# A hybrid decoder layer on Trainium2: the sums of the seven-product form as identity products on TensorE, and a new order of compression, keys and queries

## The chip, the cores and the metric

The kernel runs on one core of one Trainium2 chip. The metric is the device time of one execution in microseconds (us). The kernel before was run three times; the median is compared. The trace is of one profiled execution of the same program.

## The reference, cut to what matters

One decoder layer over 1024 tokens of width 1024, in float32:

- a SwiGLU feed-forward block (inner width 2816) on a normalised and modulated input, `u = norm(h) * a + b` with a and b from a conditioning vector, added to the residual stream h;
- a mixer on the next such u: one wide projection `u @ w_in` (queries, keys and values of sparse attention with compressed, selected and windowed branches, queries, keys, values and a gate of retention, and two merge gates), then attention (8 heads in 4 pairs), retention (8 heads in chunks of 128 tokens), and `sigmoid(ga) * (o_nsa @ w_nsa_up) + sigmoid(gb) * (o_ret @ w_ret_up)`, projected by `w_out` and added to h;
- a second feed-forward block and a final norm.

Every large product must come out at float32 quality. The kernel holds each operand as a high part (rounded to the matmul's fp32r format) and a low part (the rest), and makes one product as three: high by high, high by low, low by high (`mm3`, L275).

## The kernel before, in words

Activations lie transposed, 128 features in the partitions and tokens along the row, in two halves of 512 tokens. `u[hf]` is a pair of tiles (high, low) of 8 row blocks d for the half hf. A PSUM bank takes 512 float32 columns; `psA` has two tiles of two banks, `psO` four of one.

**The seven-product form.** Large projections are made as a 2 by 2 block product with seven block products in place of eight (a Strassen form). It needs sums of quarters of u. `combine` (L287) makes them: with b11, b21 the upper and lower four row blocks of the first half and b12, b22 those of the second, T3 = b22 - b12, T2 = b22 - t1 with t1 = b12 - b11, T4 = b21 - T2, and T1 = t1. A quarter is first put together from its high and low parts (L296, three of four on VectorE, one on GpSimd), then added (L307 and L310 on VectorE, L308 and L312 on GpSimd), then split again by `put`: ScalarE copies the high part (L300), VectorE subtracts for the low part (L301). The tile of T1 replaces b12, so that `put` comes after all plain products that read b12. `combine` runs three times: ahead of the first feed-forward block, of the mixer and of the second block. I call these places the transitions. Before each one the norm is applied: `norm_u` (L233) multiplies on VectorE (L240), adds the shift and rounds on ScalarE (L246), and makes the low part on VectorE (L248) or, for every second row block, and for every one in the first block, on GpSimd (L251, L252). Around the transition a few column tiles are made by plain products: `plain` (L498) and its gated evacuation (L478; VectorE L482 or L485), `first_proj` (L988; its gates' copy is L998) and `plain_t` (L1004). After it the weight sets follow: `wset` and `wset_n` split and combine weights (L334 to L344), `seven` (L380) empties the products (L391 to L416).

**The mixer's order** (`run`, L1491 to L1521): the first retention set, retention of four heads (`ret_core`) woven with the second retention set, retention of the other four woven with the further sets (keys, queries, merge gates), then `compress`, then sets up to the last, `keys` (L1017) woven with the last set. Keys, queries and values go through HBM: each is loaded into a staging buffer, copied to its high part on ScalarE and its low part is subtracted on VectorE (L1029 and L1030, L1056 and L1057, L1043 and L1044). Q0, the values and Q1 are loaded after the last set, ahead of `attention` (L1074).

**Attention** works per pair of heads p and token block i from 7 down to 0: scores on TensorE (L1070, L1071), mask and maximum on VectorE (L1117), exponentials on ScalarE (L1132), scaling on GpSimd (L1137), transposes on TensorE (L1159), a split on ScalarE and VectorE (L1162, L1163), products with the values (L1173). Between them stand steps of `ret_up` (L1201): first four loads of the retention output, split on ScalarE and GpSimd (L1198, L1199) through one staging buffer (t4h), then sixteen groups of 12 products. `FILL` (L31) says at which blocks a step is taken. `merge` (L1227) then makes `o_nsa @ w_nsa_up` and combines it with loads of the gates and the retention part (d_gab, 32 loads), and `out_seven` (L595) projects; its low parts are L679, its copies L678, its loads of h L633.

**What sets the order.** The code states an order, and a planner that simulates the engines (it is part of the language's compiler) may take a later instruction of a queue first when an earlier one is not ready by its own costs; `high_priority` moves instructions ahead. Each engine then works its queue in that fixed order. All DMAs but a few go through the queue of SP.

Of the kernel before, what the change touches and what calls it, by code (L numbers as in the profile page):

```python
# [17 lines left out]
P = 128  # L18
# [12 lines left out]
FILL = ((6, 5, 4), (6, 5, 3, 2, 1, 0), (6, 5, 4, 3, 2, 1), (7, 6, 5, 4, 3))  # L31
# [21 lines left out]
class Layer:  # L53
# [4 lines left out]
    def setup(self):  # L58
# [4 lines left out]
        nc.sync.dma_start(self.ident, I["k_ident"])  # L63
        self.ones = const.tile([P, P], F32, name="ones")
# [149 lines left out]
    def norm(self, i, hf, u, pool, state):  # L214

        ps = self.psA.tile([P, 2, H2], F32, name="s")
        with self.tc.high_priority():
            bc = self.norm_bc(hf, pool, ps[:, 0, :], ps[:, 1, :], state)
        u.append(self.half(hf))
        for d in range(KD):  # L220
            yield
            self.norm_u(i, hf, u, d, bc)
# [10 lines left out]
    def norm_u(self, i, hf, u, d, bc, shift=True, pool_lo=2):  # L233
# [13 lines left out]
        if d % pool_lo:  # L247
            nc.vector.scalar_tensor_tensor(ul, t, b, f32(uh), op0=ALU.add, op1=ALU.subtract)  # L248
        else:
            t2 = self.tmp.tile([P, H2], F32, name="tg", bufs=2)  # L250
            nc.gpsimd.tensor_scalar(t2, t, b, 1.0, op0=ALU.add, op1=ALU.mult)  # L251
            nc.gpsimd.tensor_sub(ul, t2, f32(uh))  # L252
# [34 lines left out]
    def combine(self, u, pool, us, first):  # L287


        nc = self.nc  # L290
        T2, T3, T4 = [tuple(pool.tile([P, 4, H2], F32R, name="t%d%s" % (i, x)) for x in "hl") for i in (2, 3, 4)]

        t1 = first.tile([P, 4, H2], F32, name="t1f")

        def quarter(eng, r, c, d, t):
            eng.tensor_add(t, f32(u[c][0][:, 4 * r + d, :]), f32(u[c][1][:, 4 * r + d, :]))  # L296
            return t

        def put(dst, d, t):
            nc.scalar.copy(dst[0][:, d, :], t)  # L300
            nc.vector.tensor_sub(dst[1][:, d, :], t, f32(dst[0][:, d, :]))  # L301

        for d in range(4):
            x = [self.tmp.tile([P, H2], F32, name=t, bufs=2) for t in ("t2", "tn", "tg")]
            b11, b12 = quarter(nc.vector, 0, 0, d, t1[:, d, :]), quarter(nc.vector, 0, 1, d, x[0])
            b22, b21 = quarter(nc.vector, 1, 1, d, x[1]), quarter(nc.gpsimd, 1, 0, d, x[2])
            nc.vector.tensor_sub(b11, b12, b11)  # L307
            nc.gpsimd.tensor_sub(b12, b22, b12)  # L308
            put(T3, d, b12)
            nc.vector.tensor_sub(b22, b22, b11)  # L310
            put(T2, d, b22)
            nc.gpsimd.tensor_sub(b21, b21, b22)  # L312
            put(T4, d, b21)
        yield
        T1 = tuple(x[:, 0:4, :] for x in u[1])
        for d in range(4):
            put(T1, d, t1[:, d, :])
        b11, b21 = [tuple(x[:, r:r + 4, :] for x in u[0]) for r in (0, 4)]
        us += [b11, b21, tuple(x[:, 4:8, :] for x in u[1]), T4, T1, T2, T3]
# [147 lines left out]
    def ffn(self, i, w_in, w_out, u, state, reg, first=None, norms=(), then=iter(()), side=()):  # L467
# [30 lines left out]
        def plain(wab, hf, f):  # L498
            pp = self.psA.tile([P, 2, H2], F32, name="s")
            for x in range(2):  # L500
                self.mm_u(pp[:, x, :], wab[x], u, hf)
            gated([pp[:, 0, :], pp[:, 1, :]], hf, f)
# [3 lines left out]
        def seven():  # L506
# [5 lines left out]
            comb = self.combine(u, pool, us, pool)  # L512
# [43 lines left out]
        else:  # L556
            ws = []
            for f in fs:
                self.sub = (nc.gpsimd, nc.vector)[f]
                ws.append(load(f))  # L560
# [456 lines left out]
    def keys(self, pool):  # L1017
# [3 lines left out]
        for b in range(2):  # L1021
            src = self.d_k[b].rearrange("(g d) t -> d g t", g=2)
            for hf in range(2):
                s = slice(hf * H2, (hf + 1) * H2)
                a = self.stage()
                for r in range(2):
                    nc.sync.dma_start(a[64 * r:64 * r + 64], src[:, :, s])
                kh, kl = self.Kh[b][:, :, s], self.Kl[b][:, :, s]
                nc.scalar.copy(kh, a)  # L1029
                nc.vector.tensor_sub(kl, a, f32(kh))  # L1030
# [15 lines left out]
    def queries(self, p, pool, stage):  # L1046
        nc = self.nc
        src = self.d_q[p].rearrange("(j d) t -> d j t", j=2)
        Q = self.Q[p] = pool.tile([P, 2, T], F32R, name="t3" + "hl"[p % 2])
        lr = slice(64, 128) if p < 2 else slice(0, 64)  # L1050
        for hf in (1, 0):
# [5 lines left out]
            nc.vector.tensor_sub(Q[lr, :, s], a[lr], f32(Q[lr, :, s]))  # L1057

# [15 lines left out]
    def attention(self, pool, sp, stage, psS, psT, psO, fill):  # L1074
# [7 lines left out]
        for p in range(4):  # L1082
            g = p // 2
            for i in range(NT - 1, -1, -1):
                if p and p < 3 and i == 7:
                    self.queries(p + 1, sp, stage)
                elif i in FILL[p]:
# [139 lines left out]
    def merge(self, onsa, mix, pool):  # L1227
        nc = self.nc
        wn = self.I["w_nsa_up"][0].rearrange("(k p) n -> p k n", p=P)
        for d in range(KD):  # L1230
            w = self.weights(wn[:, :, d * P:(d + 1) * P], [P, 4, P])
            for hf in range(2):
                s = slice(hf * H2, (hf + 1) * H2)
                a = self.tmp.tile([P, H2], F32, name="tn", bufs=2)
                nc.sync.dma_start(a, self.d_gab[d, :, s])
                b = pool.tile([P, H2], F32, name="ga", bufs=2)
# [58 lines left out]
    def run(self):  # L1295
# [56 lines left out]
        def first():  # L1352
# [51 lines left out]
            for hf in range(2):  # L1404
                for d in range(KD):
                    self.norm_u(0, hf, u, d, bcs[hf], True, 1)
# [32 lines left out]
        c_t = ExitStack()  # L1439
        sp = pool(c_n, "sevenm", "right")  # L1440
        us = []
        comb = self.combine(u, sp, us, pool(c_t, "sevenf", "right"))
# [5 lines left out]
        c_t.close()  # L1448
# [33 lines left out]
        def sets():  # L1482
# [3 lines left out]
            for d in range(KD):  # L1486
                if d == KD - 1:
                    yield "late"
# [4 lines left out]
        fill = itertools.chain(more, sets())  # L1493
        for r in range(2):
# [3 lines left out]
        with ExitStack() as c1:  # L1498
            weave(self.compress(self.keep, pool(c1, "cmp", "right")), fill, 4)
        kv = pool(c_n, "kv", "right")  # L1500
        for x in fill:
            if x == "late":
                break
        weave(self.keys(kv), fill, 2)
# [6 lines left out]
        self.Q = {}  # L1511
        self.queries(0, sp, self.stage)
# [6 lines left out]
        self.queries(1, sp, stage)  # L1519
# [79 lines left out]
```

## Time and profile before

| | |
|---|---|
| Runs (median of 3, lowest to highest) | 2398.12 us (2394.84 to 2399.73) |
| The profiled execution's own time | 2396.19 us |
| Its span, first to last instruction | 2394.4 us |
| Mean granted TensorE clock | 0.973 of full speed |
| Matmuls | 11563 |
| HBM read, written | 216.45 MB, 69.73 MB |

How to read it: the span is what the trace covers; the execution's own time is 1.8 us longer. An engine is busy while an instruction of its kind is under way; matmuls overlap, so that a busy TensorE is not one at its peak, and the count of matmuls in a stretch says more. The clock has two levels, 1.2 and 2.4 GHz; a granted clock between them is a mean over a stretch.

The stages by the trace: setup and opening of the first block to 130 us, its sets to 480, its output projection to 730, the transition to the mixer to 820, the mixer to 1260, attention to 1560, merge and output projection to 1695, the transition to the second block to 1780, its sets to 2145, output projection and final norm to the end.

### The profile page before, as it was taken

The numbers are of one execution on the slowest core, as the hardware profiler recorded it, in microseconds if no ns is written. First come the engines' busy times: TensorE is split into PE (matmuls) and PEld (weight loads), VectorE is DVE, ScalarE is ACT, GpSimd is POOL, SyncE is SP. The second block draws the span as 40 slices with busy tenths as digits, with TensorE's granted clock in tenths as the row PEclk, the third lists the DMA queues.
The fourth block names the chain that finished last, engine by engine and source line by source line (L and its number), as shares of the span: only waits on it lengthen the run. The fifth ranks groups of instructions, "written<-read, shape, count | busy, mean of one in ns | idle before, by whom it ended". The sixth has DMA issues, their size and how long they took to land.

```text
span 2394.4 us, 32603 instructions
## 1 busy us (share of the span) xinstructions
PE 2263.2 (95%) x11563; PEld 1904.2 (80%) x11563; DVE 1774.0 (74%) x2858; ACT 1054.5 (44%) x1904; POOL 1025.2 (43%) x784
## 2 busy tenths in 40 slices
PE   7799999999997899999997999999879999999998
PEld 5578888887886899887886889877668888887886
DVE  7888888668888855676757887849895555558888
ACT  4432222235774322123437876816432222235676
POOL 3755454534104544565315444530464444445202
PEclk8999999999998999999998999999899999999999
DMA  9135656374204344353544121380212222236311
GB/s 350 56 98 171 199 170 201 103 242 137 88 1 136 93 129 125 91 158 117 168 127 114 54 85 63 134 257 2 106 58 83 88 80 80 80 131 224 103 45 70
DMA packets 248886, 288.31 MB, mean 120 GB/s; under 512 B 14852, under 2 KB 169236, under 8 KB 248724
## 3 DMA queue, kind: packets, MB, share of 16 engines
q1 hardware_dynamic: 248608, 286.19, 37.6%
q8 instruction: 91, 1.49, 0.3%
q14 instruction: 71, 0.58, 0.1%
q10 hardware_dynamic: 116, 0.05, 0.0%
HBM read 216.45 MB, written 69.73 MB: 120 GB/s over the span
## 4 chain that ended last, share of the span: by engine, by line
PE 37%; DVE 6%; DMA 3%; ACT 2%; issue 1%; POOL 1%; SPq 0%; DVEq 0%; ACTq 0%; POOLq 0%
PE po L281 17%; PE po L758 5%; PE s L758 5%; PE ot L1173 3%; PE pt L1159 2%; PE s L281 2%; PE s L1070 1%; PE s L1071 1%; DMA tn<-d_gab 1%; DVE wp L679 1%; PE pt L862 1%; PE ot L1170 0%; POOL mix L1241 0%; POOL tg L251 0%; DVE pl L1163 0%
## 5 line engine op out<-in xcount | busy, mean ns | idle before, releaser
L281 PE MATMUL po<-u0h,wp 128*128 128x512 f32 x944 | 306.1, 395 | 7.3 <-DVE gates L998 4.9
L281 PE MATMUL po<-u1h,wp 128*128 128x512 f32 x880 | 282.0, 391 | 3.4 <-DVE bias L544 2.2
L758 PE MATMUL po<-wp 128*128 128x512 f32 x1128 | 268.7, 394 | 10.5 <-DVE wp L679 7.8
L758 PEld LDWEIGHTS po<-wp 128*128 128x128 f32 x1128 | 214.2, 190 | 59.3 <-DVE wp L679 10.5
L758 PE MATMUL s<-wp 128*128 128x512 f32 x1056 | 249.1, 392 | 4.1 <-DVE wp L679 2.5
L758 PEld LDWEIGHTS s<-wp 128*128 128x128 f32 x1056 | 199.1, 189 | 47.3 <-DVE wp L679 4.0
L334 ACT CAST wp<-S 128x1024 fp32r<-128x1024 f32 x98 | 103.0, 1051 | 300.4 <-PE po L281 296.4
L281 PEld LDWEIGHTS po<-u0h,wp 128*128 128x128 f32 x944 | 179.5, 190 | 46.9 <-DVE gates L998 5.1
L281 PEld LDWEIGHTS po<-u1h,wp 128*128 128x128 f32 x880 | 165.1, 188 | 40.2 <-DVE bias L544 2.6
L281 PE MATMUL po<-u0l,wp 128*128 128x512 f32 x472 | 186.1, 394 | 0.0
L463 POOL TENSOR_TENSOR t<-t,t 128x512 f32<-128x512 f32 x38 | 56.3, 1483 | 299.9 <-DVE t L407 187.9
L281 PE MATMUL po<-u1l,wp 128*128 128x512 f32 x440 | 172.5, 392 | 2.5 <-DVE u1l L243 2.5
L335 DVE TENSOR_TENSOR wp<-S,wp 128x1024 fp32r<-128x1024 f32 x98 | 158.3, 1615 | 15.5 <-ACT wp L334 15.3
L334 ACT CAST wp<-raw 128x1024 fp32r<-128x1024 f32 x98 | 82.1, 837 | 186.0 <-PE po L281 177.6
L341 POOL TENSOR_TENSOR S<-raw 128x512 f32<-128x512 f32 x49 | 69.2, 1413 | 153.2 <-DMA raw<-w_in 47.3
L281 PE MATMUL po<-t2h,wp 128*128 128x512 f32 x392 | 131.6, 396 | 2.2 <-ACT t2h L300 1.4
L281 PE MATMUL po<-t4h,wp 128*128 128x512 f32 x392 | 131.6, 396 | 1.3 <-DVE tn L399 0.7
L281 PE MATMUL po<-t3h,wp 128*128 128x512 f32 x392 | 131.8, 397 | 0.2 <-DVE t L395 0.2
L335 DVE TENSOR_TENSOR wp<-raw,wp 128x1024 fp32r<-128x1024 f32 x98 | 115.3, 1177 | 12.1 <-ACT wp L334 11.9
L395 DVE TENSOR_TENSOR t<-tn,po 128x512 f32<-128x512 f32 x57 | 39.0, 685 | 111.0 <-issue 76.9
L1163 DVE TENSOR_TENSOR pl<-pt,ph 128x512 fp32r<-128x512 f32 (+2 forms) x160 | 96.8, 619 | 11.6 <-ACT ph L1162 10.9
L251 POOL TENSOR_SCALAR tg<-tn,mod 128x512 f32<-128x512 f32 x32 | 36.6, 1149 | 160.6 <-DVE tn L240 151.5
(467 smaller groups left out, 6022.2 us busy)
## 6 DMA issues: line engine op xcount, KB each, us to landing
raw<-ffn_w_in SPq DMA_DIRECT2D x88, 512.0 KB, 4.3
raw<-ada_w SPq DMA_DIRECT2D x56, 512.0 KB, 4.3
raw<-w_in SPq DMA_DIRECT2D x40, 512.0 KB, 4.1
d_g<-t SPq DMA_DIRECT2D x50, 256.0 KB, 2.2
d_h<-hT SPq DMA_DIRECT2D x24, 512.0 KB, 5.5
hT<-d_h SPq DMA_DIRECT2D x48, 256.0 KB, 5.3
d_g<-tg SPq DMA_DIRECT2D x38, 256.0 KB, 2.0
fw<-ada_w SPq DMA_DIRECT2D x8, 1024.0 KB, 11.6
```

Source lines behind the costliest of these rows:

```text
L251: nc.gpsimd.tensor_scalar(t2, t, b, 1.0, op0=ALU.add, op1=ALU.mult)
L281: nc.tensor.matmul(ps, a, b, start=k == 0 and q == 0, stop=k == n - 1 and q == 2)
L334: nc.scalar.copy(w[:, 0], t)
L335: nc.vector.tensor_sub(w[:, 1], t, f32(w[:, 0]))
L341: nc.gpsimd.tensor_add(s[:, 0:4], b[:, 0:4], b[:, 4:8])
L395: nc.vector.tensor_add(c, u2, p)
L463: nc.gpsimd.tensor_mul(g, g, t)
L679: nc.vector.tensor_sub(w[:, x, 1], g(n[x]), f32(w[:, x, 0]))
L758: nc.tensor.matmul(po[d], l[:, e], r, start=k == 0 and z == 0 and not seeded, stop=k == m - 1 and z == 2, skip_group_check=seeded)
L1159: nc.tensor.transpose(pt[:, o + j * P:o + (j + 1) * P], a, self.ident)
L1163: nc.vector.tensor_sub(lo, pt[:, :n], f32(hi))
L1173: nc.tensor.matmul(ot, self.V2[kt // 4][:, kt % 4, b, g, :], x[:, o:o + 2 * P], start=first and m == 0, stop=last and m == 1)
```

## The change

The sums of `combine` become chains of products with the identity or its negative (`pm`, made once by ScalarE), accumulated in banks of `psA`, and `put` reads PSUM. T2 and T4 are made by adding two more products to the bank that held the sum before. All the norm's low parts go to VectorE, and the second half's row blocks are taken in the order 0, 4, 1, 5, 2, 6, 3, 7. `plain` uses `psO`. In the second block both first weight splits go to VectorE. `compress` is made before retention; keys and Q0 are loaded some sets before the last; keys are loaded into the low part's own tile; Q1 is loaded at block 5 of the first head pair. Merge gets more buffers. The three calls of `combine` lose an argument, and the pool for t1 goes.

```diff
-FILL = ((6, 5, 4), (6, 5, 3, 2, 1, 0), (6, 5, 4, 3, 2, 1), (7, 6, 5, 4, 3))
+FILL = ((6, 5, 4, 3), (6, 5, 3, 1), (6, 5, 3, 1), (7, 6, 5, 4))
...
+        self.pm = const.tile([P, 2, P], F32R, name="pm")
+        nc.scalar.copy(self.pm[:, 0], self.ident)
+        nc.scalar.mul(self.pm[:, 1], self.ident, -1.0)
...
-            self.norm_u(i, hf, u, d, bc)
+            self.norm_u(i, hf, u, d // 2 + d % 2 * 4 if hf else d, bc)
...
-        if d % pool_lo:
-            nc.vector.scalar_tensor_tensor(ul, t, b, f32(uh), op0=ALU.add, op1=ALU.subtract)
-        else:
-            t2 = self.tmp.tile([P, H2], F32, name="tg", bufs=2)
-            nc.gpsimd.tensor_scalar(t2, t, b, 1.0, op0=ALU.add, op1=ALU.mult)
-            nc.gpsimd.tensor_sub(ul, t2, f32(uh))
+        nc.vector.scalar_tensor_tensor(ul, t, b, f32(uh), op0=ALU.add, op1=ALU.subtract)
...
+        def add(ps, d, *terms):
+
+            ops = [(sign, x[d]) for sign, q in terms for x in q]
+            new = len(terms) == 2
+            for n, (sign, x) in enumerate(ops):
+                nc.tensor.matmul(ps, self.pm[:, sign], x, start=new and n == 0, stop=n == len(ops) - 1,
+                                 skip_group_check=not new)
+
+        def put(dst, d, ps, sign=1):
+            hi, lo = dst[0][:, d, :], dst[1][:, d, :]
+            if sign > 0:
+                nc.scalar.copy(hi, ps)
+                nc.vector.tensor_sub(lo, ps, f32(hi))
+            else:
+                nc.scalar.mul(hi, ps, -1.0)
+                nc.vector.scalar_tensor_tensor(lo, ps, -1.0, f32(hi), op0=ALU.mult, op1=ALU.subtract)
...
+        for d in range(0, 4, 2):
+            ps = two()
+            for x in range(2):
+                add(ps[x], d + x, (0, b12), (1, b22))
+                put(T3, d + x, ps[x], -1)
+            for x in range(2):
+                add(ps[x], d + x, (1, b11))
+                put(T2, d + x, ps[x], -1)
+            for x in range(2):
+                add(ps[x], d + x, (0, b21))
+                put(T4, d + x, ps[x])
         yield
         T1 = tuple(x[:, 0:4, :] for x in u[1])
-        for d in range(4):
-            put(T1, d, t1[:, d, :])
...
+        for d in range(0, 4, 2):
+            ps = two()
+            for x in range(2):
+                add(ps[x], d + x, (0, b12), (1, b11))
+                put(T1, d + x, ps[x])
...
         def plain(wab, hf, f):
-            pp = self.psA.tile([P, 2, H2], F32, name="s")
-            for x in range(2):
-                self.mm_u(pp[:, x, :], wab[x], u, hf)
-            gated([pp[:, 0, :], pp[:, 1, :]], hf, f)
+            pp = [self.psO.tile([P, H2], F32, name="po") for x in range(2)]
+            for p, w in zip(pp, wab):
+                self.mm_u(p, w, u, hf)
+            gated(pp, hf, f)
...
-                self.sub = (nc.gpsimd, nc.vector)[f]
+                self.sub = nc.vector
...
-                a = self.stage()
+                kh, kl = self.Kh[b][:, :, s], self.Kl[b][:, :, s]
                 for r in range(2):
-                    nc.sync.dma_start(a[64 * r:64 * r + 64], src[:, :, s])
-                kh, kl = self.Kh[b][:, :, s], self.Kl[b][:, :, s]
-                nc.scalar.copy(kh, a)
-                nc.vector.tensor_sub(kl, a, f32(kh))
+                    nc.sync.dma_start(f32(kl[64 * r:64 * r + 64]), src[:, :, s])
+                nc.scalar.copy(kh, f32(kl))
+                nc.vector.tensor_sub(kl, f32(kl), f32(kh))
...
-        Q = self.Q[p] = pool.tile([P, 2, T], F32R, name="t3" + "hl"[p % 2])
+        Q = self.Q[p] = pool.tile([P, 2, T], F32R, name="t3" + "hl"[p % 2] if p else "Q0")
...
-                if p and p < 3 and i == 7:
-                    self.queries(p + 1, sp, stage)
-                elif i in FILL[p]:
+                if (p, i) in ((0, 5), (1, 7), (2, 7)):
+                    drain(self.queries(p + 1, sp, stage))
+                for _ in range(4 if p == 0 and i == 7 else i in FILL[p]):
                     next(fill, None)
...
-                a = self.tmp.tile([P, H2], F32, name="tn", bufs=2)
+                a = pool.tile([P, H2], F32, name="ga", bufs=6)
                 nc.sync.dma_start(a, self.d_gab[d, :, s])
-                b = pool.tile([P, H2], F32, name="ga", bufs=2)
+                b = pool.tile([P, H2], F32, name="gb", bufs=5)
...
         drain(sets_ret(0))
         more = sets_ret(1)
         fill = itertools.chain(more, sets())
+        with ExitStack() as c1:
+            weave(self.compress(self.keep, pool(c1, "cmp", "right")), fill, 4)
         for r in range(2):
             with ExitStack() as c1:
                 weave(self.ret_core(r, pool(c1, "ret", "right")), fill, 1)
             drain(more)
-        with ExitStack() as c1:
-            weave(self.compress(self.keep, pool(c1, "cmp", "right")), fill, 4)
+        for _ in range(14):
+            next(fill, None)
         kv = pool(c_n, "kv", "right")
-        for x in fill:
-            if x == "late":
-                break
-        weave(self.keys(kv), fill, 2)
+        self.Q = {}
+        weave(itertools.chain(self.keys(kv), self.queries(0, kv, self.stage)), fill, 2)
         drain(fill)
...
-        self.Q = {}
-        self.queries(0, sp, self.stage)
         self.values(sp, self.stage)
...
-        self.queries(1, sp, stage)
```

## Rows read from the trace of the kernel before

**Rows 1.** The page's first part: busy us of each engine, share, instructions.

```profile
PE 2263.2 (95%) x11563; PEld 1904.2 (80%) x11563; DVE 1774.0 (74%) x2858; ACT 1054.5 (44%) x1904; POOL 1025.2 (43%) x784
```

**Rows 2.** Stretches of 10 us: busy us of each engine, matmuls, granted clock.

```profile
core 0: us, PE busy (x) PEld busy (x) DVE busy (x) ACT busy (x) POOL busy (x), PEclk, DMA share, GB/s
120.00:130.00 10.00, 10.00 (x32) 7.96 (x33) 7.60 (x5) 1.76 (x3) 10.00 (x7) 0.69 0.08 28
130.00:140.00 10.00, 10.00 (x46) 8.29 (x45) 10.00 (x11) 4.36 (x6) 5.32 (x4) 1.00 0.05 4
780.00:790.00 10.00, 6.20 (x18) 4.92 (x19) 9.96 (x9) 3.25 (x6) 9.37 (x5) 0.66 0.38 105
1770.00:1780.00 10.00, 5.28 (x16) 4.05 (x16) 10.00 (x13) 2.59 (x5) 5.03 (x3) 0.59 0.08 20
1280.00:1290.00 10.00, 9.14 (x45) 8.78 (x45) 8.71 (x42) 8.79 (x23) 9.45 (x10) 0.67 0.19 63
1620.00:1630.00 10.00, 7.96 (x23) 6.32 (x24) 10.00 (x18) 5.78 (x12) 0.00 (x0) 0.66 0.00 0
```

**Rows 3.** Waits of TensorE, 90 to 190 us: total us, times, longest.

```profile
PE s L281 <- DVE t L482: 9.1, 2, 5.1
PE s L281 <- POOL u1l L252: 2.5, 2, 1.7
```

**Rows 4.** Waits of TensorE, 745 to 830 us.

```profile
PE po L281 <- DVE gates L998: 5.4, 2, 4.9
...
PE po L281 <- ACT tn L391: 2.1, 1, 2.1
```

**Rows 5.** Waits of TensorE, 1700 to 1800 us.

```profile
PE po L281 <- DVE t2l L301: 8.7, 1, 8.7
PE s L281 <- DVE u1l L248: 1.9, 1, 1.9
```

**Rows 6.** Timeline from 130 us: start, us, engine, line; GpSimd's and VectorE's rows.

```profile
131.89 3.43 POOL L312 TENSOR_TENSOR tg<-tg,tn 128x512 f32<-128x512 f32 x2
...
134.10 1.77 DVE L301 TENSOR_TENSOR t3l<-t,t3h 128x512 fp32r<-128x512 f32 x1
135.79 0.68 DVE L301 TENSOR_TENSOR t2l<-tn,t2h 128x512 fp32r<-128x512 f32 x1
```

**Rows 7.** The page's groups: count, busy us, mean ns, idle before.

```profile
L395 DVE TENSOR_TENSOR t<-tn,po 128x512 f32<-128x512 f32 x57 | 39.0, 685 | 111.0 <-issue 76.9
```

**Rows 8.** The chain that ended last: start, us, what.

```profile
1774.72 367.02 PE po L281 x1589
```

**Rows 9.** Groups of GpSimd and VectorE, 60 to 190 us.

```profile
L251 POOL TENSOR_SCALAR tg<-tn,mod 128x512 f32<-128x512 f32 x16 | 18.5, 1167 | 9.7 <-DVE mod L160 9.0 <-DVE tn L240 0.7
...
L240 DVE SCALAR_TENSOR_TENSOR tn<-hT,ab,bcs 128x512 f32<-128x512 f32 x21 | 24.0, 1161 | 3.0 <-POOL tg L251 2.9
```

**Rows 10.** Waits of TensorE, 1255 to 1360 us.

```profile
PE s L1070 <- DVE mx L1117: 15.1, 8, 9.8
PE s L1070 <- DVE t3h L1057: 1.6, 1, 1.6
```

**Rows 11.** Timeline of VectorE from 1265 us; in brackets the idle time before.

```profile
1267.20 1.23 DVE L1044 TENSOR_TENSOR t2h<-raw,t2h 128x1024 fp32r<-128x1024 f32 x1 [2.20 <-ACT t2h L1043]
1268.67 1.22 DVE L1057 TENSOR_TENSOR t3l<-t4h,t3l 64x1024 fp32r<-64x1024 f32 x1 [0.24 <-ACT t3l L1056]
...
1272.02 0.68 DVE L1117 CUSTOM_DVE_ANT_0 u0h<-s,S 128x512 f32<-128x512 f32 x1
```

**Rows 12.** Timeline of SP's queue from 1275 us: the loads of the retention output.

```profile
1277.59 17.47 SPq L1197 DMA_DIRECT2D t4h<-d_ret  x3
```

**Rows 13.** Waits of TensorE, 1540 to 1640 us.

```profile
PE s L758 <- DVE wp L679: 2.5, 2, 2.3
...
PE po L758 <- ACT wp L678: 1.1, 1, 1.1
```

**Rows 14.** Timeline of SP's queue from 1562 us.

```profile
1565.16 7.47 SPq L633 DMA_DIRECT2D hT<-d_h  x11
```

**Rows 15.** Waits of TensorE in the mixer, 840 to 1260 us: the longest.

```profile
PE po L937 <- DVE xc L959: 1.6, 1, 1.6
```

More of the change, by code (lines that the diff above doesn't have):

```diff
@@ L231, in norm_bc, with norm_u @@
         return bc
-    def norm_u(self, i, hf, u, d, bc, shift=True, pool_lo=2):
+    def norm_u(self, i, hf, u, d, bc, shift=True):
         nc = self.nc
@@ L284, in mm_u, with combine @@
         self.mm3(ps, [((w[0][:, k, :], w[1][:, k, :]), (u[hf][0][:, k, :], u[hf][1][:, k, :])) for k in range(KD)])
-    def combine(self, u, pool, us, first):
+    def combine(self, u, pool, us):
         nc = self.nc
         T2, T3, T4 = [tuple(pool.tile([P, 4, H2], F32R, name="t%d%s" % (i, x)) for x in "hl") for i in (2, 3, 4)]
[L293 to L301, printed above, removed]
-        for d in range(4):
[L304 to L313, printed above, removed]
@@ new lines, in blocks, with two @@
+        def blocks(t, r=0):
+            return [[x[:, r + d, :] for d in range(4)] for x in t]
+        def two():
+            ps = self.psA.tile([P, 2, H2], F32, name="s")
+            return ps[:, 0, :], ps[:, 1, :]
+        b11, b21, b12, b22 = [blocks(u[c], 4 * r) for c in range(2) for r in range(2)]
+        for d in range(0, 4, 2):
[9 more added lines that the diff above has]
+                put(T4, d + x, ps[x])
@@ L314, in combine @@
         yield
         T1 = tuple(x[:, 0:4, :] for x in u[1])
-        for d in range(4):
-            put(T1, d, t1[:, d, :])
-        b11, b21 = [tuple(x[:, r:r + 4, :] for x in u[0]) for r in (0, 4)]
-        us += [b11, b21, tuple(x[:, 4:8, :] for x in u[1]), T4, T1, T2, T3]
+        for d in range(0, 4, 2):
[3 more added lines that the diff above has]
+                put(T1, d + x, ps[x])
+        q11, q21 = [tuple(x[:, r:r + 4, :] for x in u[0]) for r in (0, 4)]
@@ L321, in wset @@
+        us += [q11, q21, tuple(x[:, 4:8, :] for x in u[1]), T4, T1, T2, T3]
     def wset(self, src, ca, cb, pool):
@@ L511, in seven @@
             us = []
-            comb = self.combine(u, pool, us, pool)
+            comb = self.combine(u, pool, us)
             next(comb)
@@ L1057, in queries @@
             nc.vector.tensor_sub(Q[lr, :, s], a[lr], f32(Q[lr, :, s]))
+            yield
     def scores(self, ps, h, b, i, k0, kn, off):
@@ L1405, in first @@
                 for d in range(KD):
-                    self.norm_u(0, hf, u, d, bcs[hf], True, 1)
+                    self.norm_u(0, hf, u, d // 2 + d % 2 * 4 if hf else d, bcs[hf])
             c_f.close()
@@ L1438, in run @@
         next(gen)
-        c_t = ExitStack()
         sp = pool(c_n, "sevenm", "right")
         us = []
-        comb = self.combine(u, sp, us, pool(c_t, "sevenf", "right"))
+        comb = self.combine(u, sp, us)
         next(comb)
@@ L1447, in run @@
         drain(comb)
-        c_t.close()
         c_ps.close()
@@ L1486, in sets @@
             for d in range(KD):
-                if d == KD - 1:
-                    yield "late"
                 yield from self.set_t(self.w_in, 3352 + d * P, 4376 + d * P, us, sp, to_gate(d))
```

## The prediction

> **What bounds the kernel now.** I read the engine totals first. TensorE is busy 95% of the span, VectorE 74% and GpSimd 43% [rows 1], so in the long middle stretches only less TensorE work would help. I then cut the span into stretches of 10 us and looked for those with few matmuls. A full stretch holds 46 products of 512 columns; the poor ones lie in five places: the three transitions into the seven-product form (around 120, 785 and 1775 us), the start of attention (1260 to 1290) and the seam between `merge` and the output projection (1620) [rows 2]. Third, I asked in each place which wait ended last.
>
> In the transitions VectorE and GpSimd decide. In the first, TensorE waits 9.1 us for VectorE's gated product L482, which stands behind the sums in VectorE's queue, and 2.5 us for a low part made on GpSimd [rows 3]. In the second it waits 5.4 us for the gates' copy L998, queued behind the same sums, and 2.1 us for a PSUM bank [rows 4]. In the third it waits 8.7 us for a low part of T2 and 1.9 us for one of u1 [rows 5]. VectorE is busy 9.96 and 10.00 of 10 us there [rows 2], but partly because each of its operations is stretched: the same 512-column subtraction L301 takes 1.77 us while GpSimd's L312 runs and 0.68 us right after it [rows 6]. The Trainium skill (SBUF — State Buffer, "Who interferes with whom") says that a VectorE instruction with two SBUF inputs contends with GpSimd's reads, and one with a single SBUF input does not. By that rule the new low parts, read from PSUM and one SBUF tile, keep the short time; the trace agrees at 685 ns for L395, which reads PSUM [rows 7].
>
> After each long wait the clock falls too: at 120 us it is granted at 0.69, a mix of 1.2 and 2.4 GHz, and 32 products pass where 46 could [rows 2].
>
> **The change, part by part.**
>
> *Sums on TensorE.* Each transition gets 12 identity products for each of 4 row blocks, 48 in all; three make 144. In the longest undisturbed run 1589 products take 367.02 us, 0.231 us each [rows 8], so 33.3 us are added. If they fell wholly into idle time they would cost nothing; at the lower clock twice as much. I charge them fully, and count the idle time separately.
>
> *What goes in exchange.* VectorE loses 20 additions a transition (12 of L296, 4 of L307, 4 of L310) and GpSimd 12; the 16 low parts stay, at 0.68 us. The norm's low parts leave GpSimd (L251, 18.5 us in the first transition alone, and L252 as many times) and cost VectorE 32 more instructions, 16 of them there. The nearest row is L240, same form, 1161 ns mean under GpSimd's load [rows 9]; without that load I take 0.75, so 12 us in the first transition against more than 20 saved. That is covered: VectorE stays under TensorE's work. Waits that I expect gone: 11.6 + 7.5 + 10.6 = 29.7 us [rows 3 to 5]. The clock's loss goes with them: (46 - 32) x 0.231 = 3.2 us, 6.20 - 18 x 0.231 = 2.0 and 5.28 - 16 x 0.231 = 1.6, together 6.8 [rows 2]. That is 36.5 us.
>
> *What is late next.* The sums are a chain: products, a ScalarE copy and a VectorE subtraction of the same bank, two more products into that bank, and so on. TensorE's queue is in order, so behind a waiting product stand the plain products of the same transition, and behind those ScalarE's and VectorE's evacuations. No row shows such a round. The nearest is 2.1 us for a bank being emptied by a ScalarE copy [rows 4]. Four dependent rounds a transition (T2 and T4 for two pairs) make 12 rounds: nothing if other products always stand ready, 25 us if none do. The first transition has two columns of plain products to put between, the second most of the projection, so I take two exposed rounds, 4.2 us. `plain` now takes banks of psO, so its first product can wait for a gated one; that lies within this term. The interleaved order of u1's rows delays a first pass by at most a few products while it lets the sums begin early; I take nothing. Net of the transitions: 33.3 - 36.5 + 4.2 = **+1.0 us**.
>
> *Keys, queries, values.* At 1259 us TensorE runs dry: 1.6 us for Q0's low part and then 9.8 us [rows 10], named for L1117. VectorE's queue shows why: L1117 at 1272.02 stands behind two splits of the values and one of Q1, each held by a ScalarE copy and the load before that [rows 11]. The change loads keys into their own tile (8 loads, no staging buffer), issues Q0's 4 loads with them some 11 products before the sets end, leaves the staging buffers to the values' 2 loads, and moves Q1's 4 loads to block 5 of the first head pair. All go through SP's queue, past the last sets' weight loads, which have a full product set as cover. The 11.4 us go; of the half-clock time at 1280 (9.14 us busy at 0.67, so 3.0 us lost) [rows 2] most goes as well. The rest of the first ramp (15.1 - 9.8 = 5.3 us of waits [rows 10]) stays, because softmax's chain is the same. Four instead of three loads of the retention output stand at the front of the fill, in a single buffer; three take 17.47 us from issue to issue [rows 12]. That can hold Q1 and the first fill product. I charge 1 us: **-13.4 us**. Bounds: nothing gained to -20. The evened fill (8, 4, 4, 4 steps for 3, 6, 6, 5) moves four products' worth without adding any; nothing.
>
> *Merge.* TensorE waits 2.5 us for a low part and 1.1 us for a copy [rows 13], since the last mixed tile is late: each load of the gates has only two buffers and 11 loads of hT stand ahead on SP's queue in 7.47 us [rows 14]. Then it runs at 0.66, 23 x 0.231 = 5.3 us of work in 7.96 [rows 2]. With 6 and 5 buffers the same 32 loads run ahead. I take the 2.5 us and the clock's 2.6: **-5.1 us**; bounds nothing and -7.
>
> *The rest.* Compression before retention: the mixer's largest wait is 1.6 us [rows 15], so little can be won; its 10 loads and its chains lie under set products in both places. If that cover is thinner, perhaps 5 us. Both weight splits of the second feed-forward on VectorE: nothing.
>
> **The sum.** +1.0 - 13.4 - 5.1 = -17.5 us. The profiled execution took 2396.2 us, so 2378.7; the median of the runs is 1.9 us higher, so I forecast **2380 us**.
>
> **Rivals.**
>
> *A. The wait moves.* The start of attention keeps its gap, now behind the single buffer of retention loads. For: three such loads already span 17.47 us [rows 12], and a fourth plus Q1 stand in that line. Against: nothing before block 6 needs them. The 13.4 us are lost: 2380 + 13 = 2393.
>
> *B. Slower: the chain holds TensorE's queue.* All 12 rounds are exposed, 25 us, and each transition still loses 3.2 us to the clock, 9.6 in all [rows 2]. Then 33.3 - 36.5 + 25 + 9.6 - 13.4 - 5.1 = +12.9 us over the profiled run, 2411 on the runs' scale. It decides from where the remaining waits in the transitions pass 22 us, 7 a transition. For: the third transition has only two blocks of plain products to put between. Against: in all three there is some independent work. The Trainium skill (TensorE: Matmul & The Clock Gate, "Step-by-step: what each phase is for") says that matmuls stay in program order and only weight loads are pulled ahead; by that rule a waiting sum does hold all that is behind it. The trace agrees: during the 5.1 us wait no other product ran [rows 3].
>
> *C. More is gained.* No round is exposed (4.2), the ramp's 5.3 us shrink to half, and lower-clock stretches that I did not count go: some -10 more, 2370.
>
> *D. The order doesn't come about.* The planner places Q0 and the values after the last set, as now, and TensorE sums where VectorE's stood: the terms cancel, about 2398.
>
> **Chances.** Forecast 0.58, A 0.15, B 0.14, C 0.10, D 0.03. A measurement can tell some 0.2%, 4.8 us, from no change. Faster takes the forecast, C and half of A, 0.75; same 0.11; slower 0.14. The range runs from 2360 (C and all bounds at their good end) to 2402 (A, with some rounds exposed); most of B lies outside.
>
> **What would show it.** Right: the waits for L482, L998 and the low parts are gone, 46 products in the stretches that had 32 and 18, L301's successor at 0.7 us, GpSimd idle in the transitions, the first L1117 within 2 us of the last set product. Wrong: waits of psA's sum products for ScalarE or VectorE over 7 us a transition, a clock under 0.8 there, or TensorE waiting at attention's start for u1 or Q1.

## The result, and the profile after

| | before | after |
|---|---|---|
| median of 4 runs, us (lowest to highest) | 2396.48 (2391.23 to 2399.73) | 2382.8 (2379.0 to 2383.62) |
| ratio, 95% interval | | 0.9942 [0.9926, 0.9959] |
| profiled execution, us (span) | 2396.2 (2394.4) | 2379.0 (2377.2) |

The change gains 13.9 us (0.0058 x 2396.5). The forecast was 2380. The total was right; most of its terms were not. The first part of the profile's page of the kernel after (before: [rows 1]):

```profile
PE 2278.9 (96%) x11707; PEld 1919.4 (81%) x11707; DVE 1688.5 (71%) x2832; ACT 1054.7 (44%) x1905; POOL 860.6 (36%) x682
```

TensorE has its 144 products more, VectorE 85 us less work, GpSimd 165 us less. The waits of TensorE from 60 to 190 us, the first transition (before: [rows 3]):

```profile
engine line waited for: us in total, times, longest us
PE po L280 <- DVE u1l L247: 2.6, 3, 1.1
PE po L280 <- DVE bias L562: 1.1, 1, 1.1
PE po L280 <- ACT t L502: 1.1, 1, 1.1
PE s L298 <- DVE u1l L305: 0.7, 1, 0.7
PE s L298 <- DVE t4l L305: 0.6, 1, 0.6
```

The 9.1 us for the gated product and the 2.5 us for a GpSimd low part are gone; L298 is the new sum, and it waits 1.3 us. Next, stretches of 10 us: two that were poor before [rows 2], and two that are poor now:

```profile
core 0: us, PE busy (x) PEld busy (x) DVE busy (x) ACT busy (x) POOL busy (x), PEclk, DMA share, GB/s
120.00:130.00 10.00, 10.00 (x46) 8.20 (x45) 5.75 (x7) 3.52 (x6) 2.59 (x2) 1.00 0.45 135
1770.00:1780.00 10.00, 10.00 (x45) 8.17 (x44) 4.66 (x8) 3.84 (x6) 3.39 (x3) 1.00 0.01 2
1240.00:1250.00 10.00, 3.32 (x14) 2.09 (x12) 4.27 (x4) 4.08 (x6) 2.02 (x2) 0.88 1.08 291
1250.00:1260.00 10.00, 7.06 (x20) 5.21 (x21) 4.55 (x5) 4.42 (x5) 2.95 (x3) 0.61 0.45 146
```

The stretches from 120 and from 1770 are full, at a granted clock of 1.00. But a hole has opened at 1240 to 1260, ahead of the place where one was to close. What TensorE waits for there (1235 to 1350 us; before: [rows 10]):

```profile
PE s L1088 <- DVE mx L1135: 5.9, 8, 1.5
PE po L280 <- ACT wp L352: 5.7, 1, 5.7
PE s L1088 <- ACT Kh L1046: 3.1, 1, 3.1
```

The one wait of 9.8 us for the first softmax step is gone; the longest is 1.5. In its place TensorE waits 5.7 us for split weights of the last gate set and 3.1 us for a key copy. SP's queue tells why (timeline, columns: start us, us, engine, line, operation, tiles):

```profile
1168.86 0.59 SPq L1072 DMA_DIRECT2D raw<-d_q  x1
...
1170.14 0.58 SPq L1072 DMA_DIRECT2D raw<-d_q  x1
...
1211.09 1.24 SPq L1072 DMA_DIRECT2D raw<-d_q  x2
...
1224.76 0.38 SPq L345 DMA_DIRECT2D raw<-w_in  x1
...
1232.02 5.16 SPq L1045 DMA_DIRECT2D Kl<-d_k  x8
1237.28 0.54 SPq L1477 DMA_DIRECT2D d_gab<-t  x1
1238.55 0.33 SPq L1477 DMA_DIRECT2D d_gab<-tg  x1
1240.90 0.32 SPq L1477 DMA_DIRECT2D d_gab<-tn  x1
1241.31 0.39 SPq L345 DMA_DIRECT2D raw<-w_in  x1
```

The set's first weight load starts at 1224.76, its second only at 1241.31. Between them stand the keys' eight loads and three stores of gates. Also, Q0's loads (L1072) are staged in `raw`, the three buffers that weights are loaded into. Q0's first half takes one of them from 1168.86 on and its second half another from 1211.09, but ScalarE copies both only at 1231.55, and VectorE lets go of the last at 1236.7:

```profile
1231.55 1.99 ACT L1073 CAST Q<-raw 128x1024 fp32r<-128x1024 f32 x2
...
1233.50 1.22 DVE L1074 TENSOR_TENSOR Q<-raw,Q 64x1024 fp32r<-64x1024 f32 x1
...
1235.47 1.22 DVE L1074 TENSOR_TENSOR Q<-raw,Q 64x1024 fp32r<-64x1024 f32 x1
```

When that buffer is free, the load still stands 4.6 us behind the gates' stores. The experiments had to tell what each part of the change is worth by itself, and which of the two, the keys or Q0, holds the load.

### The profile page after: what moved, and what is told of

Its sections match the earlier page's. It is cut to its first block, busy times and chain, and to the rows that moved or that the text cites. A ratio compares the mean times of both kernels' runs of the same rounds, so it can differ in the third digit from the quotient of the medians.

```text
span 2377.2 us, 32684 instructions
## 1 busy us (share of the span) xinstructions
PE 2278.9 (96%) x11707; PEld 1919.4 (81%) x11707; DVE 1688.5 (71%) x2832; ACT 1054.7 (44%) x1905; POOL 860.6 (36%) x682
## 3 DMA queue, kind: packets, MB, share of 16 engines
q1 hardware_dynamic: 248608, 286.19, 37.8%
## 5 line engine op out<-in xcount | busy, mean ns | idle before, releaser
L280 PE MATMUL po<-u0h,wp 128*128 128x512 f32 x1008 | 323.1, 392 | 3.7 <-ACT wp L259 2.3
L280 PE MATMUL po<-u1h,wp 128*128 128x512 f32 x1008 | 323.1, 391 | 1.3 <-DVE bias L562 1.1
L280 PEld LDWEIGHTS po<-u0h,wp 128*128 128x128 f32 x1008 | 190.0, 188 | 45.1 <-ACT wp L259 2.5
L280 PEld LDWEIGHTS po<-u1h,wp 128*128 128x128 f32 x1008 | 189.2, 188 | 42.5 <-DVE bias L562 1.2
L280 PE MATMUL po<-u1l,wp 128*128 128x512 f32 x504 | 197.3, 391 | 2.6 <-DVE u1l L247 2.6
L280 PE MATMUL po<-u0l,wp 128*128 128x512 f32 x504 | 197.0, 391 | 0.0
L352 ACT CAST wp<-raw 128x1024 fp32r<-128x1024 f32 x98 | 81.9, 837 | 181.7 <-PE po L280 176.5
L280 PEld LDWEIGHTS po<-u1l,wp 128*128 128x128 f32 x504 | 94.6, 188 | 23.6 <-DVE u1l L247 3.9
L280 PEld LDWEIGHTS po<-u0l,wp 128*128 128x128 f32 x504 | 95.1, 189 | 19.5
```

What stands on the lines that cost most here:

```text
L280: nc.tensor.matmul(ps, a, b, start=k == 0 and q == 0, stop=k == n - 1 and q == 2)
L352: nc.scalar.copy(w[:, 0], t)
```

## The experiments

The times of before beside the three groups of runs were 2392.3, 2391.3 and 2390.8 us; a difference in us below is the ratio less 1 times that. Stages are compared by start times in the traces, in us: N2 is the start of the second norm's broadcast product (L230, L234 after), P2 the first product on t2h after it, M the merge's first product, N3 the third norm's broadcast product, Y the first product of the third output projection.

| kernel | ratio [95%] | to N2 | N2 to P2 | P2 to M | M to N3 | N3 to Y |
|---|---|---|---|---|---|---|
| before | 1 | 743.0 | 80.1 | 737.3 | 143.8 | 451.2 |
| after | 0.9942 [0.9926, 0.9959] | 732.7 | 82.9 | 741.4 | 133.6 | 447.3 |
| e1_sums | 0.9956 [0.9941, 0.9970] | 731.2 | 81.7 | 738.3 | 143.7 | 448.2 |
| e2_merge | 0.9978 [0.9968, 0.9987] | 741.3 | 78.4 | 739.3 | 136.1 | 453.1 |
| e3_order | 1.0027 [1.0017, 1.0038] | 740.4 | 79.4 | 744.6 | 143.8 | 452.8 |
| e4_compress | 1.0016 [1.0007, 1.0026] | 739.0 | 78.8 | 739.2 | 143.4 | 452.1 |
| e5_no_order | 0.9927 [0.9914, 0.9940] | 730.7 | 81.5 | 741.7 | 134.7 | 447.5 |
| e6_late_all | 0.9885 [0.9867, 0.9902] | 731.3 | 81.9 | 729.1 | 134.5 | 447.2 |
| e7_late_keys | 0.9910 [0.9895, 0.9925] | 729.8 | 83.8 | 738.0 | 134.5 | 447.3 |
| e8_lows_pool | 0.9952 [0.9940, 0.9964] | 735.9 | 80.0 | 735.5 | 141.6 | 447.4 |
| e9_double | 1.0114 [1.0098, 1.0130] | 744.0 | 91.7 | 742.7 | 142.3 | 458.6 |
| e10_q0_late | 0.9898 [0.9881, 0.9914] | 730.1 | 83.0 | 730.2 | 134.5 | 447.3 |
| e11_later | 0.9881 [0.9864, 0.9898] | 731.6 | 81.7 | 727.6 | 133.5 | 448.3 |
| e12_old_fill | 0.9938 [0.9922, 0.9955] | 730.0 | 84.1 | 741.0 | 133.4 | 448.3 |

The four kernels with the old sums run the same code up to N2, and reach it at 739.0 to 743.0, so that this stage of one profile is good to some 2 us. P2 to M is worse. The planner made the same program of e7 and e10, the same instructions in the same order on every engine, and of e6 and e11 too. In the first pair P2 to M still differs by 7.8 us: from 1260 to 1310 us, for one, e7's profile was granted 0.90 of the clock and e10's 1.00. So stages are read over groups of kernels, and P2 to M with the timed runs beside it.

**The three parts alone.** Each is the kernel before with one part of the change's diff.

e1_sums takes the change's hunks on `combine`, `norm_u` and the order of u1's rows, `plain`'s banks and the second feed-forward's splits:

```
-            comb = self.combine(u, pool, us, pool)
+            comb = self.combine(u, pool, us)
...
-            pp = self.psA.tile([P, 2, H2], F32, name="s")
...
+            pp = [self.psO.tile([P, H2], F32, name="po") for x in range(2)]
```

> The kernel before with the transitions' part alone: sums as identity products, the norm's low parts and the second feed-forward's splits on VectorE, plain's banks from psO, u1's rows in the new order. Theory P (the forecast's terms): +1.0 us, so about 2397 us, ratio 1.0004, with the first transition at -2 us, the second at +3, the third at 0. Rival X (the forecast was right only in total; the trace after shows the first out_seven 7 us earlier, the second transition 3 us longer, the third 4 us shorter): -6 to -10 us, ratio 0.996 to 0.9975.

-10.5 us, rival X and a little more than its -6 to -10. The four kernels with old sums (before, e2 to e4) average 740.9, 79.2 and 452.3 us in the three stages that hold a transition; the eight with the change's sums and low parts (after, e1, e5 to e7, e10 to e12) 730.9, 82.6 and 447.7. That is -10.0, +3.4 and -4.6, together -11.2 us.

e2_merge:

```
-                a = self.tmp.tile([P, H2], F32, name="tn", bufs=2)
+                a = pool.tile([P, H2], F32, name="ga", bufs=6)
...
-                b = pool.tile([P, H2], F32, name="ga", bufs=2)
+                b = pool.tile([P, H2], F32, name="gb", bufs=5)
```

> The kernel before with the merge's buffers alone (6 and 5 in place of 2 and 2). Theory P: -5.1 us, ratio 0.9979. Rival X: the whole 10 us by which the stretch from the first product of the merge to the third norm is shorter in the trace after belong to these buffers, ratio 0.9958. A third reading: half of the 10 us come from the third transition's part and show in the first run, ratio 0.998 here as in P, but with the stretch itself 5 us shorter in each.

-5.3 us by the timed runs, -3.1 to -7.7 by the interval: theory P. Its profile has M to N3 7.7 us shorter, and all kernels with the new buffers against all with the old average 134.4 against 143.1, 8.7 us. The interval and its own profile just meet; how much beyond 5 us it is stays open. The seam's stretches, first the one from 1560 us in the kernel before, then three of this run (the one from 1620 before: [rows 2]):

```profile
1560.00:1570.00 10.00, 9.58 (x30) 7.67 (x31) 3.66 (x6) 1.97 (x5) 1.30 (x1) 0.67 0.78 245
...
1560.00:1570.00 10.00, 10.00 (x36) 7.98 (x35) 3.64 (x6) 1.18 (x3) 2.35 (x2) 0.79 0.80 245
1610.00:1620.00 10.00, 10.00 (x46) 8.29 (x45) 10.00 (x18) 6.48 (x12) 0.00 (x0) 1.00 0.00 0
1620.00:1630.00 10.00, 10.00 (x46) 8.29 (x45) 7.76 (x14) 6.23 (x13) 0.00 (x0) 1.00 0.01 2
```

The stretch from 1620, which held 23 products at 0.66 before, is full. The merge's start gained too: 36 products at 0.79 where before had 30 at 0.67.

e3_order takes the hunks on compression, keys, Q0, values, Q1 and fill:

```
+        with ExitStack() as c1:
+            weave(self.compress(self.keep, pool(c1, "cmp", "right")), fill, 4)
         for r in range(2):
...
-        weave(self.keys(kv), fill, 2)
+        weave(itertools.chain(self.keys(kv), self.queries(0, kv, self.stage)), fill, 2)
```

> The kernel before with the new order alone: compression ahead of retention, keys into their own tile, Q0 with the keys, Q1 at block 5, the evened fill; sums and merge as before. Theory P: -13.4 us, ratio 0.9944. Rival X: the last gate set's second weight load stands on SP's queue behind the keys' eight loads and the gates' stores and waits for the buffers that Q0 uses, so the 11 us won at the first softmax are lost a little earlier: 0 to +6 us, ratio 1.000 to 1.0025, with TensorE waiting 5 us or more for that set's split weights.

+6.5 us (+4.1 to +9.1): rival X, just past its upper end of +6. The part that was to bring most makes the kernel slower by itself, and its trace shows the wait (1230 to 1360 us):

```profile
PE s L1070 <- DVE mx L1117: 7.5, 8, 2.5
PE po L281 <- ACT wp L334: 6.0, 1, 6.0
PE s L1070 <- ACT Kh L1028: 2.1, 1, 2.1
```

The three parts together make -9.3 us; the whole measured -13.9, with an interval of -9.8 to -17.7. Within the intervals of all four the parts add up.

e4_compress is the kernel before with the first two added lines of that diff alone (and the same two taken from behind the loop).

> The kernel before with compression ahead of retention and nothing else. Theory P: nothing (bound +5), ratio 0.999 to 1.001. Rival X: the mixer of the trace after waits 8 us for its small chains where 5 were waited before, and the lost time belongs to this move: +3 to +6 us, ratio 1.0012 to 1.0025. If this run is level, what the order loses is lost at the keys.

+3.8 us (+1.7 to +6.2): rival X, at the lower end. This run's profile does not show where: P2 to M is 739.2 against 737.3.

**What the order is worth, and what held the load.**

e5_no_order is the changed kernel without e3's hunks, so e1's and e2's together.

> The changed kernel with the order undone: sums and merge buffers new, compression after retention and keys, queries and fill as before. If the three parts add up (0.9956 and 0.9978 alone), ratio 0.9934, some 2 us faster than the changed kernel. If the order only pays together with the other parts (the whole change measured 0.9942, the three parts alone multiply to 0.9961), then 0.995 to 0.997, slower than the changed kernel.

-17.5 us: the parts add up. Against the change as it is (-13.9) the intervals overlap, so that the order cost something in the whole change rests on e3 and on what follows.

e7_late_keys and e10_q0_late are the changed kernel with one place moved:

```
-        for _ in range(14):
+        for _ in range(23):
```

> The changed kernel with keys and Q0 begun at step 91 of the fill in place of 82, nothing else. Theory X: the wait of 5.7 us for the last set's split weights and the 3.1 us for the keys' copies are gone, and the half-clock stretch behind them (20 products in the 10 us from 1250) with them: 8 to 12 us faster than the changed kernel, ratio 0.989 to 0.991. Rival: the queue is as crowded a set later and the same wait stands at the first scores, for Q0 or the keys: 0.993 to 0.996.

0.9910, 7.6 us faster than the change: theory X by its ratio, at the small end. TensorE waits neither for the set's weights nor over 1.3 us for the key copies (1225 to 1350 us):

```profile
PE s L1088 <- DVE mx L1135: 3.9, 5, 1.6
PE s L1088 <- ACT Kh L1046: 1.3, 2, 0.8
```

That moved keys and Q0 together. e10 moves Q0 alone:

```
-        weave(itertools.chain(self.keys(kv), self.queries(0, kv, self.stage)), fill, 2)
+        weave(self.keys(kv), fill, 2)
+        for _ in range(9):
+            next(fill, None)
+        weave(self.queries(0, kv, self.stage), fill, 2)
```

> The changed kernel with the keys where the change puts them (step 82 of the fill) and Q0 alone moved behind the last set's weight loads (step 99). If Q0's two staging buffers, which are two of the three that weights are loaded into, held the last load: 7 to 9 us faster than the changed kernel, ratio 0.990 to 0.992, the wait for the last set's split weights gone. If the keys' eight loads and ScalarE copies ahead of the gates' stores held it: 0.993 to 0.995, the wait still there.

0.9898, 10.5 us faster than the change. Its waits from 1230 to 1262 us:

```profile
PE s L1088 <- DVE mx L1135: 1.6, 2, 1.4
PE s L1088 <- ACT Kh L1046: 1.1, 2, 0.7
PE s L1089 <- DVE Kl L1047: 0.8, 1, 0.8
```

The wait for split weights is gone, and the weight load in question starts at 1208.47, ahead of keys and Q0. So Q0's place held it: with Q0 moved, the planner makes the same program whether the keys stand at step 82 (e10) or 91 (e7), and moving them too adds nothing. The two results are therefore one program measured twice, 7.6 and 10.5 us faster than the change. That it is the buffers, and not Q0's copies or its place in the queue, is read from the trace of after; no run gave Q0 buffers of its own.

e6_late_all is e7 with compression back behind retention. Compression and retention then use 70 steps of the fill (28 of the second retention set, 26 beside the other four heads, 16 beside compression), so that the 23 more lead to step 93 and not 91, and all of Q0 stands behind the last set's loads, which are step 99's. e11_later starts at step 100 and not 98, with Q0 behind the last set's products. It is e6 with

```
-        for _ in range(23):
+        for _ in range(30):
```

> The changed kernel with compression back behind retention and keys and Q0 begun at step 91 of the fill, so that the last set's two weight loads stand ahead of Q0's in program order. Theory X (the order loses 4 us by compression and some 9 us by the late weights): ratio 0.987 to 0.990, faster than all others. Rival: Q0 now comes late and TensorE waits for its low part instead, 0.992 to 0.995. Theory P has no cause to move: 0.994.

> The best so far (compression back, keys from step 91; 0.9885) with the keys from step 98, Q0 after the last set product. If the place at step 91 is near the best one: the last set runs undisturbed, but TensorE waits 4 to 8 us for keys and Q0 at the first scores, 0.990 to 0.992. If the less beside the last set the better: 0.986 to 0.988.

0.9885 and 0.9881, 2364.9 and 2363.2 us: theory X for e6, and the best times here, 14 us faster than the change. As the planner made the same program of both, e11 repeats e6 and tests no later place; its own question stays open. e6 against e7 is another -6.0 us for compression, -5.0 by the means of the two pairs.

e12_old_fill is e6 with before's FILL and one step a block:

```
-FILL = ((6, 5, 4, 3), (6, 5, 3, 1), (6, 5, 3, 1), (7, 6, 5, 4))
+FILL = ((6, 5, 4), (6, 5, 3, 2, 1, 0), (6, 5, 4, 3, 2, 1), (7, 6, 5, 4, 3))
...
-                for _ in range(4 if p == 0 and i == 7 else i in FILL[p]):
+                for _ in range(i in FILL[p]):
```

> The best so far (0.9885) with the fill of the kernel before: 3 loads of the retention output in the first head pair in place of 4 at its first block, 6, 6 and 5 steps after that. Theory P: the evened fill is worth nothing and the fourth load costs 1 us, so 0.988. Rival A (the loads through the single buffer hold the first fill product): 3 us or more faster, 0.986 to 0.987. If the evened fill pays, 0.990.

0.9938: 12.7 us slower than e6. The sign is that of the third reading, the size beyond all three. The products of the fill (`t4l`, the retention output's weights) up to 1345 us, first of e6 and then of this run; columns: count, shortest, median and longest ns, first and last start:

```profile
L280 PE MATMUL s<-u1h,t4l x48: 387/392/628, 1258.3 to 1342.8; 128*128 128x512 f32 x48
L280 PE MATMUL s<-u1l,t4l x24: 389/393/628, 1258.7 to 1342.6; 128*128 128x512 f32 x24
```

```profile
L280 PE MATMUL s<-u1h,t4l x8: 389/391/497, 1339.6 to 1342.2; 128*128 128x512 f32 x8
L280 PE MATMUL s<-u1l,t4l x4: 389/391/395, 1340.0 to 1342.0; 128*128 128x512 f32 x4
```

In e6, 72 products stand in the first 90 us of attention, from 1258 on; here they start at 1340 and only 12 stand there by 1345. TensorE's waits from 1252 to 1340 us in this run:

```profile
PE s L1088 <- DVE mx L1135: 7.9, 7, 2.7
PE ot L1191 <- DVE pl L1181: 2.3, 3, 1.0
PE pt L1177 <- DVE pl L1181: 2.1, 3, 1.4
PE ot L1191 <- ACT ph L1180: 1.8, 3, 1.1
```

For L1135 e6 waits 3.5 us in the same stretch. The run undoes both the four early loads and the even spread; which of the two counts more was not tried. Beside e5 (0.9927) it says one thing more: without the new fill, the new order of keys and Q0 gains nothing. By the two profiles, the gap from the last set product to the first transpose is 9.6 us shorter than in e5 (13.9 against 23.5), and from there to the merge it is 7.1 longer (289.7 against 282.6; the other kernels with the old fill have 276.6 to 283.6). What is won at the start is then waited for in the first head pair, unless products stand there. The new fill with the old order was not tried.

**Inside the transitions.**

e8_lows_pool is e1 with

```
-        nc.vector.scalar_tensor_tensor(ul, t, b, f32(uh), op0=ALU.add, op1=ALU.subtract)
+        if d % (2 if i else 1):
+            nc.vector.scalar_tensor_tensor(ul, t, b, f32(uh), op0=ALU.add, op1=ALU.subtract)
+        else:
...
+            nc.gpsimd.tensor_scalar(t2, t, b, 1.0, op0=ALU.add, op1=ALU.mult)
+            nc.gpsimd.tensor_sub(ul, t2, f32(uh))
```

> The first run (sums alone, 0.9956) with the norm's low parts left on GpSimd as before: all of the first norm's, every second of the others. Theory 1 (the sums' move brings the gain, and the low parts only follow): 0.995 to 0.997. Theory 2 (freeing GpSimd of the low parts brings it, since they delay u1 and stretch VectorE's operations in the first transition): 0.999 to 1.001, with the first transition's 9 us gone and TensorE waiting there for GpSimd's low parts.

0.9952 against 0.9956: theory 1. The move of the low parts is worth nothing that the total shows, though N2 comes 4.7 us later than in e1. What pays is the rest of e1: the sums, with the new order of u1's rows, the banks of `plain` and the second block's splits. These were not tried apart.

e9_double is e1 with

```
-            ops = [(sign, x[d]) for sign, q in terms for x in q]
+            ops = [y for sign, q in terms for y in ((sign, q[0][d]), (1 - sign, q[0][d]), (sign, q[0][d]), (sign, q[1][d]))]
```

> The first run (sums alone, 0.9956) with every pair of sum products doubled: each first half is added, taken away and added again, 144 products more, the same sums. Theory P (a product costs 0.231 us wherever it stands): +33.3 us, ratio 1.0095. If the sums fall partly into TensorE's idle time, as a rival price would have it: half, 1.0025. If the chain is the bound, more than 33 us, over 1.011.

The ratio, 1.0114, lies where the third reading put it. But against e1 it is 0.0158 x 2391 = 37.8 us, uncertain by some 5 either way, which holds theory P's 33.3 as well. The stages decide: +12.8 to N2, +10.0 to P2 and +10.4 from N3, 33.2 us for 144 products, the 0.231 us of theory P; the rest lies mostly between P2 and M, where no sum stands. The added sums found no idle time to fall into, and the chain did not stretch with them: the sum products wait 0.3 us for L305 in the first transition, and not at all in the others.

## Why the prediction was right in sum and wrong in its terms

**Sums, +1.0 forecast, -11.2 in the profiles and -10.5 timed.** The price of the products held (e9). The exposed rounds nearly held: the change's sum products and what follows them wait 1.3 us for L305 in the first transition, 1.7 in the second, nothing in the third, 3.0 in place of 4.2. By transition my terms made -2.3, +3.0 and +0.3; measured -10.0, +3.4 and -4.6. The step that failed is "Waits that I expect gone: 11.6 + 7.5 + 10.6": I took one or two waits by name in each place, and one stretch of low clock. In the first transition, before leaves TensorE idle 19.5 of 130 us, and its clock takes some 5.8 more (10 us at 0.69, 10 at 0.83, 2.7 at 0.62); e1 is idle 4.6, all of it at 1.00. The difference, 20.7, less 11.1 for 48 products, is 9.6 of the 10.0 (e1 by itself reaches N2 11.8 earlier). In the 100 us from N3, before loses 13.6 us idle and 5.9 to the clock, e1 1.6 and 4.0; less 11.1 that is 2.8 of the 3.0 us by which e1 is shorter there. So in both places more idle time went than the named waits, and in the first more of the clock's loss than the one stretch, 5.8 for 3.2. The first transition's two windows, before and e1, in two lines each:

```profile
60.00:130.00 70.00, 55.86 (x278) 43.60 (x277) 60.13 (x57) 26.57 (x37) 57.59 (x40) 0.90 0.16 52
130.00:190.00 60.00, 54.68 (x230) 43.86 (x229) 52.60 (x54) 20.35 (x30) 31.74 (x20) 0.97 0.40 123
```

```profile
60.00:130.00 70.00, 65.41 (x338) 52.83 (x338) 56.12 (x74) 31.72 (x46) 11.28 (x7) 1.00 0.24 78
130.00:190.00 60.00, 60.00 (x267) 48.75 (x266) 36.70 (x43) 17.82 (x25) 16.36 (x12) 1.00 0.35 111
```

**Attention's start, -13.4 forecast.** The gap itself shrank as said: from the end of the last set product to the first transpose of the probabilities 22.7 us before, 9.7 after, so -13.0. But from P2 to that last set product it is 436.5 before and 453.7 after, 17.2 more; with attention itself even, P2 to M is 4.1 us longer. The order alone, timed, costs 6.5 (e3). The step that failed is "All go through SP's queue, past the last sets' weight loads, which have a full product set as cover". That set's second load came 16.5 us after its first, because of Q0's place (e10), by the trace because Q0's staging held the buffers. 7.6 to 10.5 us hang on it; the two waits of 5.7 and 3.1, with 2.8 us of clock behind them (7.06 us at 0.61), make 11.6. My sign, "the first L1117 within 2 us of the last set product", came true (0.6 us) and proved nothing, since it is measured from an event that had itself moved.

**The evened fill, 0 forecast, 12.7 us measured** (e12 against e6). "Moves four products' worth without adding any; nothing" counted products and not what they cover. The rest of the first ramp, forecast to stay at 5.3 us, did so in the change (5.9 us for L1135, 1235 to 1350 us); from 1252 to 1340 it is 3.5 in e6 and 7.9 without the fill. Without this fill the order of the keys gains nothing (e12); whether the fill gains without the order was not tried.

**Compression, 0 with a bound of +5.** +3.8 alone, 5.0 to 6.0 by e6 and e11 against e7 and e10: the bound was the value. After waits 8.1 us in the mixer (830 to 1235 us) where before waits 4.9 (830 to 1240), the most for retention's transposed keys and a set's sum:

```profile
PE pi L946 <- ACT kT L940: 2.7, 2, 1.5
PE po L280 <- DVE tn L417: 2.2, 2, 1.2
PE po L955 <- DVE xc L977: 1.1, 1, 1.1
```

That this is the price was read from traces, not tried.

**Merge, -5.1 forecast, -5.3 timed**: right, by the seam's waits and clock; the profiles' 8.7 hold the merge's start too, which I left out.

**Rivals.** B is out: 3.0 us of waits in the chain, where 22 were needed. Of C one part came in the first transition: lower clock that I had not counted, 2.6 us. Of A the title came, "The wait moves": attention's gap closed, and a new one opened ahead of it, by Q0's staging and not behind the retention loads. So 2380 was met by luck: the transitions' term was forecast 12 us too high, the start's some 18 too low, and the two nearly cancelled (-11.2 for +1.0; P2 to M 4.1 longer for 13.4 shorter).

## What to carry to other kernels

Price a stall by the stretch's idle time and granted clock, not by the largest waits by name: the small ones go with it. When loads move earlier, follow the buffers that they are staged in: if these are shared with another stream, that stream's next load waits for the moved tile's last reader. Where freely placed products stand can matter though their number stays the same: without 60 of 72 of them under a softmax's start, the new order of its loads brought nothing. And look whether two versions of the code come out as two programs before their times are compared.

## What the runs showed of the hardware

How far VectorE is stretched beside GpSimd goes by where its operands lie. The same multiplication of the norm in e8, where GpSimd makes low parts, and in after, where it does not, with the new low part L308 of after and, last, the old one L301 of before (group rows: busy us, mean ns):

```profile
L244 DVE SCALAR_TENSOR_TENSOR tn<-hT,ab,bcs 128x512 f32<-128x512 f32 x32 | 33.5, 1070 | 4.2 <-POOL tg L255 3.5 <-PE bc L234 0.5
L244 DVE SCALAR_TENSOR_TENSOR tn<-hT,ab,s 128x512 f32<-128x512 f32 x32 | 22.8, 745 | 10.9 <-PE s L234 7.4 <-POOL tg L255 3.4
```

```profile
L244 DVE SCALAR_TENSOR_TENSOR tn<-hT,ab,bcs 128x512 f32<-128x512 f32 x32 | 24.8, 797 | 0.8 <-PE bc L234 0.5
L244 DVE SCALAR_TENSOR_TENSOR tn<-hT,ab,s 128x512 f32<-128x512 f32 x32 | 22.8, 743 | 12.7 <-PE s L234 12.6
L308 DVE SCALAR_TENSOR_TENSOR t2l<-s,t2h 128x512 fp32r<-128x512 f32 x12 | 8.2, 686 | 4.3 <-ACT t2h L307 4.2
```

```profile
L301 DVE TENSOR_TENSOR t2l<-tn,t2h 128x512 fp32r<-128x512 f32 x12 | 16.7, 1395 | 0.1
```

With both tensors in SBUF (hT, bcs) it takes 1070 ns beside GpSimd's work and 797 without; with one in PSUM (s) 745 and 743, although 26 of e8's 32 ran beside GpSimd for most of their time. The new low part L308, from PSUM, takes 686 ns where L301 averaged 1395 for T2's. So the 0.68 us of the forecast held. The Trainium skill (SBUF — State Buffer, "Who interferes with whom") says that a VectorE instruction with two SBUF inputs contends with GpSimd's reads and one with a single SBUF input does not; both pairs agree.

Not expected: the 4.7 us by which e8 reaches N2 later than e1 do not show in its time; the later stages are shorter by 0.8 to 2.8 us each, which one profile can hardly tell from nothing, and why was not tried.
